# Delta rule's recurrence: four ticks a chunk instead of three, with half ticks between its products

## The chip, the cores and the metric

One Trainium2 chip, one core. The metric is the device time of one execution, in microseconds, over several runs. In the rows of the profile PE is TensorE (PEld its weight loads), DVE VectorE, ACT ScalarE, POOL GpSimd, SP SyncE, whose queue issues the DMAs (SPq).

## The reference, cut to what matters

One decoder layer over 2048 tokens: a projection, two token mixers with four heads each, an output projection, an MLP, a gated embedding. The change concerns one mixer, the gated delta rule. Its state S (128 x 128 for each head) goes from chunk to chunk:

```python
def step(s, inp):
    u_n, w_n, qk_n, qg_n, kt_n, cd_n = inp
    v_new = u_n - w_n @ s                       # u, w: solves of a triangular system of the chunk
    o = qg_n @ s + qk_n @ v_new
    s = s * cd_n + kt_n.T @ v_new
    return s, o
```

The second mixer (HGRN2) has a recurrence of the same kind without the solve.

## The kernel before, in words

All is computed transposed, features by tokens, with tokens in four quarters q of 512. In the mixers' stage (the loop from line 1008 on) the outer work is the input projection: for each quarter one piece "ab" and then, for each of four heads h, eight pieces (`works`). A piece is one bank of 128 x 512 summed over 24 products (line 1020, rows `mm`). It is cut into three *ticks* (`SPT = 3`) of eight products each. After each eight products `tick()` is called: it looks up in `agenda` the generators that are due at this count of the clock, and lets each issue its next step. So the mixers' small products are strewn among the projection's large ones. A head of both mixers starts every 24 ticks (27 where a new quarter starts), and its steps take some 60, so two to three heads are under way at any time.

The gated delta rule's head (`gdn_mixer`, from line 562 on) is such a generator, and the list `A_STEPS` says at which ticks after the head's start its steps are due. In order, with the tick in brackets: load of the decays, keys turned and normed (7 to 9), `kk` products giving u, qk, and the scaled y_kg and y_qg (10), values turned and the store `ud` of the triangular blocks (12), their load `sys` (14), solve of the 32 x 32 blocks on VectorE (16 to 23, tiles pr and xs, lines 653 to 663), store `xd` and loads `xt` (24, 26), transpose to `xn` (28), the merging products psp, psx, psd (30 to 36), then the recurrence, three ticks a chunk, four chunks (38 to 49):

- first product `psa` (line 724): needs the state S; VectorE makes `r` of it (line 726);
- second product `psb` (line 729): needs r; ScalarE makes `w` of it (line 731);
- third product `psc` (line 734): needs w; VectorE makes the next S (line 736); right behind it two products into the output bank `pso` (lines 737, 738).

Each step is one tick from the one before, also psc to the next chunk's psa. After that `finish` (from line 540) takes eight steps (50, 52, 54, 56, 57, 58, 60, 61): og and its squares; the norm's sum `nrm` on TensorE and the DMA `sd`; the load of `m` (line 267); a power of m, on VectorE and GpSimd; the store `rd` (line 273); the broadcast load `rsb` (line 234); the gated og; its store `mixd` (line 555).

Steps of several heads share a tick: at a head's ticks 40 to 47 the next head's solve (its 16 to 23) is due, at 38 the next head's sys load, at 60 and 62 the ud store and the sys load of the head after next. The second mixer's head (`hgrn_mixer`) runs its levels at 24 to 38, a turn at 40, its own recurrence at 42 to 45 and its finish from 46 (`B_STEPS`). The very last head, (3,3), has lists of its own (`A_LAST`, `B_LAST`). After the last piece the clock goes on with tiles of an embedding, six products each, a tick behind each.

TensorE's order is the program's, written by hand as above, and in this stage so is SP's. The order of VectorE, ScalarE and GpSimd is made by a planner that runs through the program with its own costs and issues what is ready; it may bring work forward. SP issues its DMAs strictly in order and waits at each for its data or buffer; the weights of each piece are reloaded (`w`, line 180) at the piece's start, once the piece three before has freed the buffer.

## Time and profile before

| | |
|---|---|
| median of 3 runs | 2773.16 us (2772.43 to 2774.76) |
| the profiled execution's own time | 2769.21 us |
| its span, first to last instruction | 2767.3 us |
| mean granted TensorE clock | 0.993 |
| TensorE busy, share of the span | 2680.7 us, 97% |
| VectorE busy | 2044.9 us, 74% |
| ScalarE busy | 1469.9 us, 53% |
| DMA, mean | 213 GB/s |

A row of a timeline gives the start, the duration, engine, line, operation and what is written from what; in brackets the idle time of the engine just before and what ended it. Successive matmuls overlap in the pipeline, so their distance is read from start to start. A row of the waits gives who waited for whom: total in us, times, longest.

### The profile page before, as it was taken

Reading aid. Unit: us, or ns where it says so; the run is one execution under the profiler, and the core shown is the slowest. Engines: PE = TensorE matmul, PEld = TensorE weight load, DVE = VectorE, ACT = ScalarE, POOL = GpSimd, SP = SyncE. Lnnn points to the kernel's source line nnn. Section 1 sums busy time; section 2 is a strip of 40 time slices with the busy share of each in tenths; the row PEclk is TensorE's granted clock in tenths of the full one; section 3 lists DMA queues with packets and bytes.
Section 4 is the critical chain, followed back from the end, with each engine's and each line's share of the span. In section 5 each row is a group of like instructions: output and inputs, shape, how many; then the busy total and the mean of one; then the engine's idle time right before and its main releaser. Section 6 shows DMA issues by size and latency. Waiting matters only on the chain.

```text
span 2767.3 us, 38374 instructions
## 1 busy us (share of the span) xinstructions
PE 2680.7 (97%) x12721; PEld 2215.3 (80%) x12721; DVE 2044.9 (74%) x4242; ACT 1469.9 (53%) x2943; POOL 104.2 (4%) x104
## 2 busy tenths in 40 slices
PE   6999999999999999999999999999999999999999
PEld 4788788788888887777788888887888888887887
DVE  6788877787787677578889867857787765567775
ACT  6665555455546445575555646545454445465431
POOL 0000000000000000000000000001000000001000
PEclk9999999999999999999999999999999999999999
DMA  7776777667666665887466447667454356577663
GB/s 261 255 250 217 235 247 247 219 209 250 220 213 202 214 227 170 278 276 258 140 214 224 172 175 237 225 193 239 157 191 162 135 175 203 194 254 240 214 206 121
DMA packets 268598, 589.24 MB, mean 213 GB/s; under 512 B 55642, under 2 KB 59960, under 8 KB 249200
## 3 DMA queue, kind: packets, MB, share of 16 engines
q1 hardware_dynamic: 268400, 586.79, 63.6%
q8 instruction: 101, 1.65, 0.3%
q14 instruction: 97, 0.79, 0.1%
HBM read 419.75 MB, written 166.92 MB: 212 GB/s over the span
## 4 chain that ended last, share of the span: by engine, by line
PE 61%; DVE 15%; DMA 10%; issue 7%; ACT 4%; SPq 1%; POOL 1%; DVEq 0%; POOLq 0%; ACTq 0%
PE u L1090 22%; PE d L1090 20%; PE mm L1020 9%; PE mmg L1090 6%; DVE pr_g L658 2%; DMA ud_g<-u_g 2%; DMA sys_g<-ud_g 2%; DVE xs_g L661 1%; DVE xs_g L663 1%; PE mmo L1090 1%; DMA raw_out<-in_w_out_dram 1%; DVE xt L160 1%; DMA rd_g<-m_g 1%; DMA cache_in<-w 1%; DMA rsb_g<-rd_g 1%
## 5 line engine op out<-in xcount | busy, mean ns | idle before, releaser
L1020 PE MATMUL mm<-xt,w 128*128 128x512 f32 x3072 | 770.0, 399 | 3.3 <-ACT qk_h L758 1.6
L1020 PEld LDWEIGHTS mm<-xt,w 128*128 128x128 f32 x3072 | 559.5, 189 | 109.8 <-ACT qk_h L758 2.0
L1090 PE MATMUL d<-db,da 128*128 128x512 f32 x2688 | 615.3, 391 | 5.6 <-ACT db L212 3.7
L1090 PE MATMUL u<-t,wu 128*128 128x512 f32 x2604 | 603.7, 393 | 3.3 <-ACT wu L159 3.3
L1090 PEld LDWEIGHTS d<-db,da 128*128 128x128 f32 x2688 | 506.3, 189 | 113.9 <-ACT db L212 5.0
L1090 PEld LDWEIGHTS u<-t,wu 128*128 128x128 f32 x2604 | 488.7, 188 | 117.6 <-ACT wu L159 4.1
L213 DVE TENSOR_TENSOR db<-db 128x512 fp32r<-128x512 f32 x224 | 161.4, 720 | 75.2 <-ACT db L212 74.3
L1419 DVE TENSOR_TENSOR u<-u,u 128x512 f32<-128x512 f32 x224 | 150.3, 682 | 71.8 <-PE u L1090 70.6
L212 ACT ACTIVATE db<-db 128x512 fp32r<-128x512 f32 x224 | 140.8, 629 | 83.2 <-DMA db<-hid 77.8
L1090 PE MATMUL mmo<-mixT,w_out 128*128 128x512 f32 x720 | 171.7, 399 | 8.9 <-DVE w_out L160 6.4
L1090 PE MATMUL mmg<-h2T,wg 128*128 128x512 f32 x768 | 177.4, 393 | 0.0
L1460 ACT ACTIVATE u<-u 128x512 f32<-128x512 f32 x128 | 80.8, 632 | 176.4 <-DVE u L1419 176.1
L1090 PEld LDWEIGHTS mmo<-mixT,w_out 128*128 128x128 f32 x720 | 137.1, 191 | 42.5 <-DVE w_out L160 8.2
L1090 PEld LDWEIGHTS mmg<-h2T,wg 128*128 128x128 f32 x768 | 144.2, 188 | 32.9
L160 DVE TENSOR_TENSOR da<-da 128x512 fp32r<-128x512 f32 x128 | 93.0, 727 | 87.1 <-ACT da L159 86.9
L159 ACT ACTIVATE da<-da 128x512 fp32r<-128x512 f32 x128 | 80.4, 628 | 134.9 <-DMA da<-sumd 111.3
L159 ACT ACTIVATE wu<-a 128x512 fp32r<-128x512 f32 x124 | 73.9, 622 | 50.6 <-DMA a<-in_w_up_dram 49.2
L658 DVE TENSOR_TENSOR pr_g<-xs_g,sys_g 128x16 f32<-128x16 f32 (+14 forms) x240 | 93.8, 391 | 5.3
L223 POOL TENSOR_TENSOR acc_y<-acc_y,sq_y 128x512 f32<-128x512 f32 x28 | 38.5, 1374 | 1392.8 <-ACT sq_y L222 1392.0
L160 DVE TENSOR_TENSOR wu<-a,wu 128x512 fp32r<-128x512 f32 x124 | 84.7, 686 | 3.6 <-ACT wu L159 3.5
L1461 ACT ACTIVATE u<-u 128x512 f32<-128x512 f32 x128 | 80.8, 631 | 3.7
L160 DVE TENSOR_TENSOR da<-dr,da 128x512 fp32r<-128x512 f32 x96 | 66.2, 690 | 18.5 <-ACT da L159 16.8
(374 smaller groups left out, 3800.9 us busy)
## 6 DMA issues: line engine op xcount, KB each, us to landing
w<-cache_in SPq DMA_DIRECT2D x96, 1024.0 KB
db<-hid SPq DMA_DIRECT2D x224, 256.0 KB
cache_in<-w SPq DMA_DIRECT2D x32, 1024.0 KB
hid<-u SPq DMA_DIRECT2D x128, 256.0 KB
da<-sumd SPq DMA_DIRECT2D x128, 256.0 KB
a<-in_w_up_dram SPq DMA_DIRECT2D x124, 256.0 KB
hid<-ht SPq DMA_DIRECT2D x96, 256.0 KB
dr<-in_w_down_dram SPq DMA_DIRECT2D x96, 256.0 KB
```

What stands on the lines that cost most here:

```text
L159: S.activation(t[:, 0], raw, AF.Copy)
L160: eng.tensor_tensor(t[:, 1], raw, t[:, 0], ALU.subtract)
L212: S.activation(t[:, 0], plain(t), AF.Copy)
L213: V.tensor_tensor(t[:, 1], plain(t), t[:, 0], ALU.subtract)
L223: eng.tensor_tensor(acc, acc, sq, ALU.add)
L658: V.tensor_tensor(pr[:, :, :, 0:i], xs[:, None, :, 0:i].broadcast_to([P, 2, GC, i]), sys[:, 0:i, i : i + 2].rearrange("p j two -> p two j" ...
L661: V.tensor_reduce(xs[:, :, i : i + 2].rearrange("p g two -> p two g"), pr[:, :, :, 0 : i + 1], AX.X, ALU.add)
L1020: PE.matmul(ps, *terms[i], start=i == 0, stop=i == nt - 1)
L1090: PE.matmul(ps, a, b, start=start, stop=stop)
L1419: V.tensor_tensor(c[new], c[old], ps, ALU.add)
L1460: S.activation(c[k], c[k], AF.Relu)
L1461: S.activation(c[k], c[k], AF.Square)
```

## The change

A chunk takes four ticks. psa stands at a whole tick, psb one and a half ticks later, psc one tick after psb, and the next psa one and a half ticks after psc; the four chunks stand at 38, 42, 46 and 50. The finish follows from 53 to 64 with the distances it had. So that a step can be due at a half, `half()` lets the steps of the clock less a half go; it is called in the middle of each eight products, and in the tail, where embedding tiles take the place of the pieces, right before each tick. The lists of the last head are as they were.

```diff
 A_STEPS = ((3, 6, 7, 8, 9, 10, 12, 14) + tuple(range(16, 24)) + (24, 26, 28, 30, 32, 34, 36)
-           + tuple(range(38, 50)) + (50, 52, 54, 56, 57, 58, 60, 61))
+           + tuple(o for c in range(38, 54, 4) for o in (c, c + 1.5, c + 2.5))
+           + (53, 55, 57, 59, 60, 61, 63, 64))
...
         clock[0] += 1
+
+    def half():
+
+        for gen in agenda.pop(clock[0] - 0.5, ()):
+            next(gen, None)
...
                 for s in range(SPT):
                     for i in range(s * nt // SPT, (s + 1) * nt // SPT):
+                        if i == (2 * s + 1) * nt // (2 * SPT):
+                            half()
                         PE.matmul(ps, *terms[i], start=i == 0, stop=i == nt - 1)
...
                     next(outs, None)
+                half()
                 tick()
```

## The prediction

> **What bounds the kernel now.** I read the page first, then the busy time of the stage that the change touches (145 to 1145 us: the recurrences of all sixteen heads, of which the change touches fifteen), then who waits for whom there, and last the timelines of single heads. A head is called by (q, h), times are us from the span's start.

> ```profile
> PE 2680.7 (97%) x12721; PEld 2215.3 (80%) x12721; DVE 2044.9 (74%) x4242; ACT 1469.9 (53%) x2943; POOL 104.2 (4%) x104
> ```
> ```profile
> 145.00:1145.00 1000.00, 966.84 (x5302) 823.16 (x5301) 769.33 (x2193) 541.93 (x1375) 56.25 (x63) 1.00 0.68 224
> ```
> TensorE sets the time: busy for 97% of the span, at the full granted clock in this stage (the 1.00). The change moves products of TensorE but adds and removes none, so all it can win or lose is TensorE's idle time. In the stage that is 1000 less 966.84, 33 us (second row; columns after the window: its length, then busy time of PE, PEld, DVE, ACT, POOL). VectorE is busy for 77% there.

> ```profile
> PE psb_g L729 <- DVE r_g L726: 17.3, 18, 2.6
> ...
> PE psa_g L724 <- DVE S_g L736: 4.5, 4, 1.5
> PE psp_g L682 <- DVE xn_g L677: 2.4, 3, 0.8
> ```
> These rows give the total wait, its count and the longest. Two thirds of the 33 us are the recurrence's own: psb waits for r (17.3) and psa for the state (4.5), both made by VectorE. TensorE takes its products in order, so behind a waiting psb stand all the projection's products. psc, which waits for ScalarE's w, is not in the list at all.

> **What a wait costs, and the distances.** Head (2,1) runs almost without waits:

> ```profile
> 743.37 0.39 PE L734 MATMUL psc_g<-w_g,kt_g 128*128 128x128 f32 x2
> 743.60 0.39 PE L737 MATMUL pso_g<-y_qg,S_g 128*128 128x128 f32 x2
> ...
> 746.34 0.38 PE L724 MATMUL psa_g<-S_g,y_kg 128*128 128x128 f32 x2
> 746.48 2.07 PE L1020 MATMUL mm<-xt,w 128*128 128x512 f32 x8
> 748.39 0.39 PE L729 MATMUL psb_g<-r_g,xt_full 128*128 128x128 f32 x2
> ...
> 762.73 0.39 PE L724 MATMUL psa_g<-S_g,y_kg 128*128 128x128 f32 x2
> ```
> Two small products take 0.22 to 0.23 from start to start, and psa to psb, with a tick's eight large products between, 2.05; so a half tick (four) is 0.92. Breaking the stream once more costs nothing that these rows show: 2.05 is 0.22 and eight products of 0.229. For the 120 places in fifteen heads that move to a half tick I take zero (bounds: 0.02 us either way at each, 2.4 us in all). The eight large products (start 746.48, 2.07) overlap the next start by 0.16, so a wait loses 0.16 more than its idle time, and 0.10 more in the restart (0.49 against 0.39 in the waits below): 22 waits, 21.8 + 22 x 0.26 = 27.5 us. That is the most that can be won.

> **What goes.** Some waits are a distance a little too short. One of chunk 0, in (0,3), TensorE and VectorE:

> ```profile
> 342.74 0.39 PE L724 MATMUL psa_g<-S,y_kg 128*128 128x128 f32 x2
> ...
> 347.65 0.49 PE L729 MATMUL psb_g<-r_g,xt_full 128*128 128x128 f32 x2 [0.94 <-DVE r_g L726]
> ```
> ```profile
> 347.26 0.34 DVE L726 SCALAR_TENSOR_TENSOR r_g<-vt_g,inv_g,psa_g 128x128 f32<-128x128 f32 x1
> ```
> psb can start 0.39 after r starts, here 4.91 after psa. Undisturbed the distance is 2.5 (psa's pair 0.22, four small products of a level 0.44, eight large ones 1.83), with the half tick 3.4: 1.5 stays. Others are of another kind. (3,0), again TensorE and VectorE, and VectorE's total wait of this sort in the stage:

> ```profile
> 938.22 0.39 PE L734 MATMUL psc_g<-w_g,kt_g 128*128 128x128 f32 x2
> ...
> 945.66 0.49 PE L729 MATMUL psb_g<-r_g,xt_full 128*128 128x128 f32 x2 [1.34 <-DVE r_g L726]
> ...
> 960.35 0.39 PE L724 MATMUL psa_g<-S_g,y_kg 128*128 128x128 f32 x2
> ```
> ```profile
> 940.01 0.23 DVE L663 SCALAR_TENSOR_TENSOR xs_g<-xs_g,sys_g 128x4 f32<-128x4 f32 x1 [2.96 <-DMA sys_g<-ud_g]
> ...
> 959.77 0.34 DVE L736 SCALAR_TENSOR_TENSOR S_g<-S_g,cd_g,psc_g 128x128 f32<-128x128 f32 x1
> ```
> ```profile
> DVE xs_g L663 <- DMA sys_g<-ud_g: 21.6, 11, 3.5
> ```
> VectorE stood still for 2.96 us because sys_g, the next head's triangular blocks, had not landed; then it works through the next head's solve without a pause, and r and S lie in that row of work. Five heads, (0,1), (0,2), (1,1), (1,2) and (3,0), are late in this way. To them belong the four waits of psa (4.5) and five of psb, the last of them the 1.34 above, together by my reading about 7.4: with 0.26 for each of the nine, 14.2 of the 27.5.

> In these five the half tick helps little, because VectorE, not the distance, sets the pace up to about tick 47. Old: chunk 0's psc to chunk 3's psa (ticks 40 to 47) takes 19.36 in (2,1) and 22.13 in (3,0); 2.77 are lost. New: chunk 2's psa stands at tick 46, its psb at 47.5. Up to that psb TensorE has the same work as up to old chunk 3's psa, less a psb (0.22) and a psc with its two outputs (0.67, three pairs), plus a half tick (0.92): 19.4. Its r takes the place that the state update of tick 46 has in VectorE's row today, 959.77. So psb can't start before 960.16, and its turn is at 938.22 + 19.4 = 957.62: 2.54 is still lost, 0.2 won. The same rows of the other four give 0.2 to 1.1; I take 0.6 for each of the five, 3 in all.

> The waits of the first kind are the remaining 13.3. In the four heads that wait at chunk 0 (the first shown, the last (2,3)) about 2.5 stay; chunk 3's go, since its psb moves from tick 48 to 51.5, when the solve is through; for chunk 2, whose psb now bears the end of the solve, I leave 2.3. Won: 8.5.

> **What is added.** The finish (norm, gate, store) comes three ticks later, with all it issues: the sd store at tick 55, the m load at 57, the rd store at 60, the rsb load at 61, mixd at 64. VectorE's share of it, with chunk 3's r and S, moves into ticks 50 to 53, ahead of the transpose for psp (tick 54). psp's wait of 2.4 could grow; 48 to 62 is where VectorE is least pressed, so I take 1 (bounds 0 and 8, half a microsecond a head). Operands that are needed longer (y_kg to tick 50, rewritten at 52; y_qg to 52.5, rewritten at 55) keep two ticks, 4 us; were that used up, ScalarE's write would wait, not TensorE. In (3,2) the last two chunks fall among the embedding's tiles of six products (1.4 by the 0.229 above), where a half tick stands right before the next tick: 0, at most 1.

> The SP queue is the delicate part. At tick 60 it issues the ud store of the head after next, and at 62 the sys load that was late above. (3,0) today:

> ```profile
> 981.81 0.32 SPq L180 DMA_DIRECT2D w<-cache_in  x1
> 984.55 0.32 SPq L273 DMA_DIRECT2D rd_g<-m_g  x1
> ...
> 987.04 0.32 SPq L234 DMA_DIRECT2D rsb_g<-rd_g  x1
> 991.33 0.32 SPq L180 DMA_DIRECT2D w<-cache_in  x1
> 991.75 1.80 SPq L638 DMA_DIRECT2D ud_g<-u_g  x4
> ...
> 997.21 0.54 SPq L647 DMA_DIRECT2D sys_g<-ud_g  x1
> ```
> ```profile
> 522.62 0.32 SPq L180 DMA_DIRECT2D w<-cache_in  x1
> 523.03 0.38 SPq L273 DMA_DIRECT2D rd_g<-m_g  x1
> ```
> rd (tick 57 today) will stand ahead of ud, behind the weights' reload of tick 60. If m is done by then, as in (1,1) (last two rows), ud is later by one issue, 0.42 (991.33 to 991.75). That is the low end; the high end, 2.7, is a rival. I take 0.42, since m's data are loaded three ticks ahead. The five late heads pay it whole, 2.1; of the other ten half, 2. The rsb load then waits for rd's landing ahead of sys: 987.04 less 984.55 is 2.5, and sys waits 5.5 from ud's issue anyway (991.75 to 997.21), so that is covered.

> Those 5.5 us decide whether sys is late at all. [...] The measured 5.5 decides.

> **Sum.** 3 + 8.5 won, 1 + 2.1 + 2 lost: 6.4 us. The profiled execution took 2769.21; it would take 2763. The median of the runs shown, 2773.16, is 4 us above it, so 2767.

> **Rivals.** *Full relief*: the planner, which orders VectorE's work anew, puts r and S ahead of the solve's steps, and nearly all of the 27.5 goes; less the 5 lost, 2751. For it: a distance of 1.5 ticks exceeds most of the delays. Against it: the solve itself is late. *The wait only moves*: the solve's end decides everywhere, and psb of chunk 2 loses what psb of chunks 1 and 3 lost; 2773, no change. *The SP queue turns it round, slower*: in (3,0) rd is issued 2.74 after the reload of its work (981.81 to 984.55), because m was not done. Moved rigidly by three ticks it keeps ud back by 2.7. sys lands later by as much, and VectorE starts the solve later. The five late heads lose 2.7 each, 13.5. The others have a reserve, in (2,1):

> ```profile
> 761.49 0.34 DVE L736 SCALAR_TENSOR_TENSOR S_g<-S_g,cd_g,psc_g 128x128 f32<-128x128 f32 x1
> ```
> 761.49 + 0.40 against 743.37 + 19.4 leaves 0.9, so ten heads lose 1.8 each, 18. Less the 11.5 won, with the 1 for psp: 21 slower, 2794, if every head meets it; if half do (and half pay the low end), about 7, 2780. I take the middle, 2787. It decides from a delay of about 1.3 us on (5 x 1.3 and 10 x 0.4, and the 1, are the 11.5 won). For it: the rigid shift. Against it: (1,1), where rd follows its reload at once. A change that does nothing is excluded: fifteen heads use these steps; the last has its own.

> **Chances.** Forecast 0.42 (2767, own range 2761 to 2772, 0.25 of it below 2767.6), full relief 0.12, only moved 0.13, SP queue 0.28, another order of VectorE that costs time 0.05. The range 2752 to 2788 leaves out the ends of full relief and of the queue. What a measurement can tell from no change is 0.2%, 5.5 us. Faster by more: 0.25 and full relief, 0.37; within it: the rest of the forecast and the moved waits, 0.30; slower by more: 0.33.

> **What would show it.** Right: psb's wait for r falls from 17.3 to about 9, psa's from 4.5 to under 2, what is left of psb's lies in chunk 2 of the five late heads; the rd store stands less than 1 us behind its reload; VectorE's wait for sys_g stays under 30. Wrong, to the fast side: psb's wait under 4. Wrong, to the slow side: sys_g above 40, ud more than 1.3 us behind the reload, and the waits of psb, psa and psp together above 28.

## The result, and the profile after

The changed kernel takes 2782.38 us (median of six runs, 2779.64 to 2787.36) against 2772.80 for the kernel before (six runs): ratio 1.0029, 95% interval 1.0018 to 1.0039. It is slower by 0.3%, where the prediction said 0.2% faster. The profiled execution took 2780.50 us, span 2778.7 (before 2767.3), mean granted clock 0.990 (before 0.993). It is not one execution alone: the six runs of the changed kernel have a granted clock of 0.988 to 0.991, those of the kernel before in the experiments below, on three chips, 0.991 to 0.996.

Changed lines have moved: psa is L730, r L732, psb L735, w L737, psc L740, S L742; the projection's products are L1028. The page's busy times and the stage from 145 to 1145 us, after:

```profile
PE 2688.3 (97%) x12721; PEld 2223.5 (80%) x12721; DVE 2045.3 (74%) x4242; ACT 1469.2 (53%) x2943; POOL 105.5 (4%) x104
```
```profile
145.00:1145.00 1000.00, 965.13 (x5258) 825.65 (x5257) 765.24 (x2184) 536.07 (x1369) 55.39 (x62) 0.99 0.67 221
```

TensorE runs the same 12721 products but is busy 7.6 us longer, and the stage's granted clock is 0.99 where it was 1.00. TensorE's waits from 145 to 1165 us (total, times, longest; the rows of before that the prediction shows are the same up to 1165):

```profile
PE ps_gb L485 <- DVE gbb L482: 13.0, 3, 4.4
PE pso_h L847 <- DVE S_h L846: 10.8, 9, 2.6
PE at_h L819 <- DVE qk_h L825: 3.1, 1, 3.1
PE psc_g L740 <- ACT w_g L737: 2.8, 5, 0.8
...
PE psa_g L730 <- DVE S_g L742: 1.1, 2, 0.6
...
PE psb_g L735 <- DVE r_g L732: 0.5, 2, 0.3
```

The waits that the change was to shorten are gone: psb's fell from 17.3 to 0.5 us, psa's from 4.5 to 1.1. Two others have come, neither of which stands in the list of before: the second mixer's pso_h waits 10.8 us for its state S_h (more on it below), and ps_gb 13.0 in only three waits. ps_gb belongs to a step not told of so far. `decays` computes a quarter's decays: its first step makes gb with a scan on VectorE, its third copies half of gb into gbb on VectorE (L482) and transposes gb and gbb on TensorE into ps_gb (L485). It is put on the clock from the piece "ab" with the offsets (0, 2, 4, 5), so the third step of quarter q falls on tick 99q + 6. That is tick 54 of head (q-1, 2), whose finish stood at 50 and 52 and now begins at 53 and 55. VectorE, then TensorE, at the first border, after:

```profile
315.73 1.35 DVE L475 TENSOR_TENSOR_SCAN gb<-one,sp 4x128 f32<-4x128 f32 x4
...
318.42 0.66 DVE L551 TENSOR_TENSOR og_g<-pso_g,zt_zg 128x512 f32<-128x512 f32 x1
...
320.60 0.67 DVE L161 TENSOR_TENSOR hl_g<-osq_g,hl_g 128x512 fp32r<-128x512 f32 x1
...
323.25 0.27 DVE L482 COPY gbb<-gb 36x256 f32<-36x256 f32 x1
```
```profile
323.58 0.32 PE L485 MATMUL ps_gb<-cst,gbb 36*128 36x36 f32 x1 [4.32 <-DVE gbb L482]
...
324.04 3.78 PE L1028 MATMUL mm<-xt,w 128*128 128x512 f32 x8
```

The same place before:

```profile
310.59 0.69 DVE L545 TENSOR_TENSOR og_g<-pso_g,zt_zg 128x512 f32<-128x512 f32 x1
...
319.13 1.35 DVE L469 TENSOR_TENSOR_SCAN gb<-one,sp 4x128 f32<-4x128 f32 x4
...
321.58 0.30 DVE L476 COPY gbb<-gb 36x256 f32<-36x256 f32 x1
```
```profile
322.36 0.23 PE L479 MATMUL ps_gb<-cst,gbb 36*128 36x36 f32 x1
```

Before, the finish's og started 8.5 us ahead of the scan, and the transposes ran without a wait. After, gb is ready at 317.1 (315.73 + 1.35), but the planner puts the finish's og, its squares and their split, and with them steps of a convolution and of the second mixer, ahead of the small copy gbb, which starts only at 323.25. Of these 6.2 us the finish's three steps take 1.8; why the planner puts the convolution's, which stood behind the copy before, ahead of it as well, no run shows. TensorE, which takes its products in order, stands for 4.32 us. It waits in the same way at 587.24 (4.35) and 852.94 (4.38).

Then comes what the trace of before does not show in this stage at all. The same border in windows of 3.41 us (start and end, length, busy time of PE, PEld, DVE, ACT, POOL, granted clock, DMA):

```profile
318.09:321.50 3.41, 1.17 (x10) 0.93 (x8) 3.41 (x8) 2.13 (x8) 0.00 (x0) 0.99 1.14 341
321.50:324.91 3.41, 1.33 (x5) 1.17 (x6) 3.07 (x9) 1.97 (x4) 0.00 (x0) 0.50 0.85 294
324.91:328.33 3.42, 3.42 (x9) 2.65 (x9) 3.01 (x7) 0.41 (x2) 0.00 (x0) 0.51 0.84 278
328.33:331.74 3.41, 3.41 (x22) 3.03 (x22) 0.81 (x3) 1.68 (x5) 0.00 (x0) 1.00 0.18 25
```

The clock is halved from 321.50 to 328.33, 6.8 us: the eight large products at 324.04 take 3.78 us, those of the prediction's rows 2.07. Between 70 and 1165 us the kernel before has no such stretch, the changed one has 30.7 us of them: 6.8 at the first and the third border, 3.4 at the second, 3.4 behind pso_h's longest wait at 818.33, and three of 3.4 at 126.9, 1109.9 and 1120.2.

The sum, from the two traces: TensorE's idle time from 70 to 1165 us (stretches over 0.05 us) goes from 36.8 (42 waits) to 39.6 us (31 waits), +2.8. For the halved clock I take, as an estimate, half of the time within the 30.7 us in which TensorE works, +13.1. Outside this stage the same two terms give -3.9 (clock) and +1.1 (idle). The four add up to 13.1, where the spans differ by 11.4; the remaining 1.7 I can't place. So the total wait hardly changed. It was concentrated in fewer and longer waits, and those cost the clock as well.

### The profile page after: what moved, and what is told of

It is laid out like the page before. It is cut to its first block, busy times and chain, and to the rows that moved or that the text cites. A ratio compares the mean times of both kernels' runs of the same rounds, so it can differ in the third digit from the quotient of the medians.

```text
span 2778.7 us, 38391 instructions
## 1 busy us (share of the span) xinstructions
PE 2688.3 (97%) x12721; PEld 2223.5 (80%) x12721; DVE 2045.3 (74%) x4242; ACT 1469.2 (53%) x2943; POOL 105.5 (4%) x104
## 4 chain that ended last, share of the span: by engine, by line
PE 48%; DVE 5%; DMA 3%; ACT 2%; issue 2%; SPq 0%; POOL 0%; DVEq 0%; ACTq 0%; POOLq 0%
PE u L1099 22%; PE d L1099 19%; PE mmg L1099 6%; PE mmo L1099 1%; DMA da<-sumd 1%; DMA xo<-in_xT_dram 0%; DVE w_out L161 0%; DVE t L161 0%; DMA db<-hid 0%; DMA raw_out<-in_w_out_dram 0%; PE mme L187 0%; DMA b<-h1d 0%; ACT da L160 0%; DVE acc_o L224 0%; ACT L1136 0%
## 5 line engine op out<-in xcount | busy, mean ns | idle before, releaser
L1028 PE MATMUL mm<-xt,w 128*128 128x512 f32 x3072 | 796.0, 404 | 2.3 <-ACT qk_h L764 1.6
L1028 PEld LDWEIGHTS mm<-xt,w 128*128 128x128 f32 x3072 | 558.8, 191 | 103.9 <-ACT qk_h L764 2.0
```

The costliest lines, as they stand in the source:

```text
L1028: PE.matmul(ps, *terms[i], start=i == 0, stop=i == nt - 1)
```

## The experiments

Each time is given as a ratio to the kernel before on the same chip, since chips differ (medians of before: 2767.59 for the first four runs, 2772.59 for the next three, 2768.59 for the last two).

**The border's copy alone: two ticks later.** The third and fourth step of `decays` are moved out of the finish's way, from the second quarter on.

```diff
-                        at(clock[0], decays(ps, q), (0, 2, 4, 5))
+                        at(clock[0], decays(ps, q), (0, 2, 6, 7) if q else (0, 2, 4, 5))
```

> The changed kernel with one shift: the step of the quarter's decays that copies gbb and turns ps_gb comes two ticks later (from the second quarter on), away from the tick at which the moved finish puts its norm on VectorE. Theory A (the recurrence's waits are gone, but VectorE's row at the quarter's border is fuller, TensorE waits 4.3 us for gbb three times, and its clock is halved behind these waits): the three ps_gb waits (13.0 us) fall under 3, the half-clock stretches at 321, 588 and 850 go, the time falls by 15 to 20 us, to 2762 to 2768, below the kernel before. Theory B (breaking the large products' stream at half ticks costs about 0.1 us at each of 120 places, 10 us in all): only the 13 us of wait go, less what moves on, 2770 to 2773. Theory C (SP's queue, rd ahead of ud): nothing at the border matters, 2778 to 2783.

Measured: 2759.13 us, ratio 0.9968 (0.9956 to 0.9981). The waits from 145 to 1165 us, and the place at the first border:

```profile
PE pso_h L847 <- DVE S_h L846: 7.3, 7, 1.9
```
```profile
321.00 0.28 DVE L482 COPY gbb<-gb 36x256 f32<-36x256 f32 x1
```
```profile
322.45 0.23 PE L485 MATMUL ps_gb<-cst,gbb 36*128 36x36 f32 x1
```

ps_gb's waits are gone, idle time is 22.9 us, the halved clock 10.2. The copy comes no sooner: it starts 7.9 us behind the scan (313.13 to 321.00), in the changed kernel 7.5; it is TensorE that comes to it later. One pair of offsets in another function turns the change from 0.3% slower to 0.3% faster than the kernel before. psb's and psa's waits stay as small as in the changed kernel (0.5 and 0.9), so the recurrence keeps its gain, and it was the border that took it back.

**The late finish alone.** The kernel before, with its old recurrence, but the finish three ticks later:

```diff
-           + tuple(range(38, 50)) + (50, 52, 54, 56, 57, 58, 60, 61))
+           + tuple(range(38, 50)) + (53, 55, 57, 59, 60, 61, 63, 64))
```

> The kernel before with its recurrence at ticks 38 to 49, and only the finish moved to 53 to 64. Theory A: the recurrence's waits for r and S stay (about 22 us), the wait for gbb at the three borders comes (8 to 13 us) and the clock falls behind it: 10 to 20 us slower than before, 2783 to 2793. Theory B: no half ticks, so no slower, 2771 to 2775. Theory C: the queue order is that of the changed kernel, so 8 to 12 us slower, but with sys_g later and no wait for gbb.

Measured: 2778.1 us, ratio 1.0034 (1.0021 to 1.0046), as slow as the whole change, with no half tick in it.

```profile
PE psb_g L729 <- DVE r_g L726: 18.7, 25, 1.6
PE psp_g L682 <- DVE xn_g L677: 5.6, 4, 2.3
...
PE ps_gb L479 <- DVE gbb L476: 2.4, 1, 2.4
```

The collision takes different forms at the three borders: ps_gb waits 2.38 at 320.30, psp 2.28 at 582.92 and 2.29 at 844.72. Idle time is 38.6 us, only 1.8 more than before, and the clock is halved for 13.7 us (318.9 to 325.8 and 844.6 to 851.4). So psp's wait, which the prediction had named, does grow, but at the borders, not in every head. With psp's 0.8 at the first border the waits at the borders are 7.8 us, against 2.4 before (psp alone) and 13.0 in the changed kernel: the late finish makes a collision by itself, but not the whole of it. Nor is the equal time made up in the same way: here psb's waits have stayed.

**Control: the same shift in the kernel before.**

> Control for the first run: the kernel before with the decays' step two ticks later. All theories: its ps_gb waits are 4.6 us in two cases, so 0 to 5 us faster, 2768 to 2773. If it gains as much as the first run, that run says nothing of the finish.

Measured: 2766.56 us, ratio 0.9994 (0.9985 to 1.0002). The shift gains nothing that can be told where the finish does not stand in its way. (The 4.6 us that the expectation counts are two waits of quarter 0, at 61.6 and 64.7 us, which the shift leaves as they are; at the borders ps_gb did not wait before.) So the 0.3% of the first experiment are the change's own, not the shift's.

**Work in place of the wait.** The changed kernel, with 24 products of a size that fills the wait, whose result nothing reads, ahead of the border's transposes:

```diff
             ps = bank(f"ps_gb_{q}", ph)
+            for i in range(24 if q else 0):
+                PE.matmul(ps[:, NC * 36 :], xts[q][i % KD][:, 0, :P], xts[q][i % KD][:, 1, NC * 36 :],
+                          start=True, stop=True)
```

> The changed kernel with 24 products of 368 columns (about 4 us of TensorE's time, results read by nobody) ahead of ps_gb at the three borders, so that TensorE is busy where it waited for gbb. Theory A: the wait is as long but is no idling, the half-clock stretches at 321, 588 and 850 (17 us, 8.5 us of loss less what the wait covers) go, so 3 to 8 us faster than the changed kernel, 2774 to 2779, although work was added. If the clock had no part: the same as the changed kernel or slower, 2780 to 2786.

Measured: 2771.42 us, ratio 1.0014 (1.0002 to 1.0026).

```profile
317.65 4.25 PE L485 MATMUL ps_gb<-xt 128*128 128x368 f32 x24
...
322.50 0.25 PE L488 MATMUL ps_gb<-cst,gbb 36*128 36x36 f32 x1 [0.42 <-DVE gbb L482]
```

The border takes as long as with the wait (4.25 of work and 0.42 against 4.32), and the halved clock goes from 30.7 to 3.4 us. So it is TensorE's idling that is followed by the halved clock, not the border's length. The time is 1.0014 against 1.0029, some 4 us less, with intervals that overlap; by the sum above it should be 11, and the last projection product starts 5.8 earlier (1089.4 against 1095.2). That the clock stays up is shown; that this saves time is likely, and its size stays open.

**Half the shift.** One tick instead of two:

```diff
-                        at(clock[0], decays(ps, q), (0, 2, 4, 5))
+                        at(clock[0], decays(ps, q), (0, 2, 5, 6) if q else (0, 2, 4, 5))
```

> The changed kernel with the decays' last two steps one tick later (offsets 0, 2, 5, 6) instead of two. If the border's wait is a distance: a tick with its products (2 us) comes off each of the three waits of 4.3 to 4.4, leaving 2 to 2.5 each, and the clock is halved behind those of the three whose idle time falls by more than 1.7 us into one of the gate's windows of 3.4 us (none of the nine traces so far has a halved stretch begin behind less than 1.72, or a full one go on behind more than 1.69): ratio 0.998 to 1.001, between 1.0029 and 0.9968. If the gain of the two ticks comes from another order on VectorE and not from the distance: the waits stay at 4 and the ratio at 1.003, or they vanish at once and the ratio is 0.997.

Measured: 2762.73 us, ratio 0.9980 (0.9971 to 0.9989).

```profile
PE ps_gb L485 <- DVE gbb L482: 4.7, 3, 1.6
```
```profile
319.41:322.82 3.41, 1.84 (x11) 1.47 (x11) 3.03 (x11) 2.90 (x5) 0.00 (x0) 1.00 1.04 316
322.82:326.24 3.42, 3.42 (x15) 3.13 (x14) 2.71 (x6) 1.03 (x4) 0.00 (x0) 0.50 1.05 292
```

It lies between, as a distance would: each of the three waits is 1.57 us, 2.8 less for one tick. Behind two of the three the clock was halved (322.8 and 582.2), behind the third (842.26) not. Ahead of the first of them stood 1.57 us of idle time in one window (3.41 less 1.84), less than the 1.7 that the expectation gives. No run shows the gate that it speaks of; what the traces show of its windows stands in the last section.

**Do the halves matter?** With the shift, the recurrence on whole ticks:

```diff
-           + tuple(o for c in range(38, 54, 4) for o in (c, c + 1.5, c + 2.5))
+           + tuple(o for c in range(38, 54, 4) for o in (c, c + 2, c + 3))
```

> The changed kernel with the decays' shift (offsets 0, 2, 6, 7 from the second quarter on), and in it the recurrence on whole ticks: psa at c, psb at c + 2, psc at c + 3, the next psa at c + 4. Tells whether the halves matter or only that a chunk has four ticks. If the distance of each pair of products decides: psb's wait for r stays under 1 us, but psc to the next psa is one tick again, as in the kernel before, where psa lost 4.5 us, so psa loses 3 to 5 and the ratio to the kernel before is about 0.998. If only the four ticks count (the solve ends by then, whichever product waits): psa under 1.5 us and the ratio 0.9968 as with the halves. If breaking the eight products in the middle costs 0.1 us each, which the late finish alone spoke against: 0.993.

Measured: 2758.05 us, ratio 0.9949 (0.9930 to 0.9967).

```profile
PE psa_g L730 <- DVE S_g L742: 8.9, 12, 2.2
...
PE pso_h L847 <- DVE S_h L846: 2.9, 2, 1.5
```

psa's wait comes back, more than expected (8.9 us), and pso_h's goes down by 4.4; idle time is 23.7 us against 22.9 with halves. The two can't be told apart in time. A chunk's fourth tick counts, and where in it the products stand does not show.

**The second recurrence spread.** With the shift and the halves:

```diff
-B_STEPS = (..., 38, 40, 42, 43, 44, 45, 46, ...)
+B_STEPS = (..., 38, 40, 41, 42.5, 44, 45.5, 46, ...)
```

> The changed kernel with the decays' shift, and the second mixer's recurrence spread from ticks 42, 43, 44, 45 to 41, 42.5, 44, 45.5. If pso_h's wait for S_h (7.3 us with the shift alone) is a distance too short by about a half tick: it falls under 3, the halved clock behind it at 803 us goes, and the ratio is 0.995. If S_h is late because VectorE is behind with its whole row: the wait stays at 5 to 8 and the ratio at 0.9968.

Measured: 2761.07 us, ratio 0.9963 (0.9951 to 0.9975).

```profile
PE psc_g L740 <- ACT w_g L737: 5.3, 5, 2.3
PE psa_g L730 <- DVE S_g L742: 3.6, 6, 1.2
...
PE psb_g L735 <- DVE r_g L732: 2.9, 6, 0.9
...
PE pso_h L847 <- DVE S_h L846: 0.9, 2, 0.5
```

pso_h's wait goes as expected (7.3 to 0.9), the time does not: psc, psa and psb lose 11.8 us where they lost 4.0. So pso_h's wait was a distance too short, and the waits change places; halved stretches in the stage, 3.4 us where there were 10.2, and idle time, 26.8 where it was 22.9, about cancel.

**The old steps in head (3,2), whose end lies in the tail**, added to this:

```diff
                 a_steps, b_steps = (A_LAST, B_LAST) if (q, h) == (NQ - 1, 3) else (A_STEPS, B_STEPS)
+                if (q, h) == (NQ - 1, 2):
+                    a_steps = A_OLD
```

> As the one with the spread second recurrence, and head (3,2), whose last two chunks fall among the embedding's tiles, takes the steps of the kernel before. If the two stretches of halved clock in the tail (3.4 us each near 1086 and 1096 us) come of the three ticks that its finish is later there: they go, and the ratio is lower by 0.001 (some 3 us) than without. If they come of the last head alone: no difference.

Measured: 2760.04 us, ratio 0.9959 (0.9943 to 0.9974). The last halved stretch of the stage, behind at_h's wait of 3.1 us, goes. The gain of 0.001 that was expected can't be told at these intervals.

**All together, on whole ticks.**

> Everything found so far together: four ticks a chunk on whole ticks (psa c, psb c + 2, psc c + 3), the decays' shift (0, 2, 6, 7), the second recurrence at 41, 42.5, 44, 45.5, and the steps of the kernel before in head (3,2). If what each took away stays away: no halved clock between 70 and 1165 us, TensorE idle under 22 us there, ratio 0.9945. If the waits only change places, as they did with the spread second recurrence alone: idle 23 to 27 and ratio 0.996, no better than the shift alone.

Measured: 2754.48 us, ratio 0.9948 (0.9936 to 0.9961), the lowest found beside the whole ticks' 0.9949, 0.5% below the kernel before and 0.8% below the change as it was made (0.9948 / 1.0029).

```profile
145.00:1145.00 1000.00, 976.54 (x5353) 832.68 (x5352) 779.23 (x2200) 544.64 (x1386) 55.63 (x64) 1.00 0.68 227
```

Idle time from 70 to 1165 us is 27.8, in 39 waits of which none is over 1.9, and no stretch of halved clock lies between 71 and 1165 us: more wait than with the shift alone, and no more time. The idle time that I expected (under 22) did not come; the ratio did. That it beats the shift alone (0.9968) is not shown, since the intervals overlap.

## Why the prediction was wrong, step by step

- **What can be won.** Nearly all of psb's and psa's 21.8 us of waiting went, but not all of that was won. psc and pso_h, which did not wait before, wait 13.6 together, and 9.9 with the border freed (the first experiment). So the 21.8 became 15.2, and 11.3 there. In the late heads VectorE does set the pace, as forecast, but what is left of the wait does not stand in front of psb. In (3,0), from the start of tick 40 (938.22 in the prediction's rows; now the second mixer's turn t_hkh, since psc stands half a tick later):

```profile
947.67 0.60 PE L538 MATMUL t_hkh<-cst,qk_h 128*128 128x128 f32 x4
...
956.44 0.49 PE L847 MATMUL pso_h<-qk_h,S_h 128*128 128x128 f32 x2 [0.85 <-DVE S_h L846]
...
969.00 0.49 PE L735 MATMUL psb_g<-r_g,xt_full 128*128 128x128 f32 x2 [0.20 <-DVE r_g L732]
```
```profile
948.69 0.23 DVE L669 SCALAR_TENSOR_TENSOR xs_g<-xs_g,sys_g 128x4 f32<-128x4 f32 x1 [2.19 <-DMA sys_g<-ud_g]
...
956.04 0.34 DVE L846 SCALAR_TENSOR_TENSOR S_h<-S_h,gg_h,pss_h 128x128 f32<-128x128 f32 x1
...
968.60 0.34 DVE L732 SCALAR_TENSOR_TENSOR r_g<-vt_g,inv_g,psa_g 128x128 f32<-128x128 f32 x1
```

  VectorE's row from the solve's start to r takes 19.91 us, where the row to the state update took 19.76 (940.01 to 959.77): it stayed, as assumed, and r comes 0.6 earlier, since the solve starts 0.77 earlier against tick 40 (1.02 behind it, before 1.79). psb starts 21.33 behind tick 40, so 1.9 are lost against the undisturbed 19.4, where the forecast had 2.54. But only 0.20 of them are psb's own wait.

  TensorE had been held up before, mainly at pso_h, which needs S_h, and S_h is made in the same row of VectorE. Before, psc and its outputs stood between two steps of the second mixer, 3.19 us from one to the next (945.99 to 949.18); moved away, they leave 2.53 (952.67 to 955.20), and S_h comes too late. The spread second recurrence, which lengthens this distance, bears it out (7.3 to 0.9).

  Over all fifteen heads TensorE takes 309.4 us from tick 40 to psb of chunk 2, where it took 304.8 before to the product in that place (psa of chunk 3), and 305.8 with the border freed. So in these ticks nothing was won, and the rival *the wait only moves* was right there, with another product than it named; what was won lies at chunks 0 and 3, the waits of the first kind. The 3 us for the five late heads were too many by the traces of before as well: worked like (3,0), the other four give 0.0 to 0.5 each, not 0.2 to 1.1.
- **The finish's move, 1 us (bounds 0 and 8).** This is the step that failed and, with the clock, turned the sign. The prediction looked at who waits for VectorE in ticks 50 to 53 of the same heads (psp, which it put at 1 and whose wait went from 2.4 to 0.5) and called those ticks the least pressed. It did not list the steps of other generators at 53 to 57: the gbb copy of `decays`, once a quarter, with TensorE behind it. That is 13.0 us of waiting in three places, outside the bounds. With the copy's step out of the way the changed kernel is 8.5 us faster than the kernel before (7.4 faster than the kernel before with the same shift), where 6.4 were forecast; that it comes so near is in part luck, since the terms of that sum did not come out one by one.
- **The clock.** The 1.00 of the stage was quoted and then taken as given. The waits were priced at their idle time and 0.26 each, read from waits of which none had halved the clock. The term that was missing comes to 13.1 us, by the estimate above.
- **The SP queue.** The rival that ended on the slow side was not the mechanism. In (3,0) rd stands right behind its reload, and ud behind rd, at the low end of the bounds; of the other heads from 345 us on, three have ud 1.6 to 2.2 behind the reload, the rest under 1:

```profile
1000.00 0.32 SPq L181 DMA_DIRECT2D w<-cache_in  x1
1000.37 0.42 SPq L274 DMA_DIRECT2D rd_g<-m_g  x1
1000.88 1.94 SPq L644 DMA_DIRECT2D ud_g<-u_g  x4
```
```profile
DVE xs_g L669 <- DMA sys_g<-ud_g: 16.1, 12, 3.6
```

  VectorE's wait for sys_g fell from 21.6 to 16.1; the prediction's bound of 30 held. The 5.5 us that it reads from ud's issue to sys are not all ud's landing: the four issues of ud take 1.8 of them, and two other stores hold the queue up to 995.87, so that sys could have gone 1.3 earlier at most.
- **The half ticks at nothing.** Nothing speaks against it: with the border freed the kernel with half ticks is 8.5 us faster than the kernel before, and the whole ticks are not measurably better.
- **Head (3,2) in the tail, 0, at most 1.** at_h waits 3.1 us there, with a halved stretch behind it. With the old steps in this head that wait goes, but another of the tail's comes back (mme for ScalarE's sq_e, 1.5 to 5.0), and the time can't be told apart.
- **The signs named beforehand.** Psb under 4 was to be the sign of the fast side. It came true, and the kernel was slower: the signs watched the waits that the change touches, and the time went to waits of other heads' steps and to the clock. A rival "the wait moves to another generator's step" was missing; the *wait only moves* of the prediction had it at the solve's end.

## What to carry over

A step that is moved takes all its work on every engine past the steps of whatever else is due at those ticks: list these, the rare ones too (here a copy once a quarter), and ask of each what TensorE has queued behind it. Waits on a busy TensorE need not be worth their sum: from 70 to 1165 us the kernel before has 42 of them, 36.8 us, the longest 2.60, and no halved clock; the changed one has 31, 39.6 us, three of them of 4.3 to 4.4, and 30.7 us of halved clock. So a change that leaves the total as it is and concentrates it can be slower. A product taken out of a tick shortens that tick for the others in it, whose own waits may then appear (here 3.19 us became 2.53, and pso_h's waits came). And where a wait vanishes, count the waits behind the same engine's work before calling it won: here about half of it stood in front of another product.

## What the runs showed of the hardware

The length of a wait does not tell in these traces whether a halved stretch follows; what goes with it is how much of one window is idle. The traces of before and after, from 70 to 1165 us, have 631 windows at full clock. In seven of them, all in the changed kernel, TensorE is idle for 1.9 to 3.1 us, and a halved window follows each; in the others it is idle for 1.7 at most, and none follows. Less was followed by one in the late finish alone, 1.78 (3.41 less 1.63, from 315.50 to 318.91), and in half the shift, the 1.57 above. So these runs give no one limit. The two longest waits of pso_h in the changed kernel show how a wait falls into windows:

```profile
550.08:553.49 3.41, 1.79 (x9) 1.32 (x7) 3.34 (x9) 1.26 (x2) 0.00 (x0) 1.00 0.66 246
553.49:556.90 3.41, 2.65 (x15) 2.30 (x16) 3.41 (x8) 0.37 (x1) 0.00 (x0) 1.00 0.73 216
```
```profile
816.41:819.82 3.41, 1.49 (x9) 1.33 (x10) 3.41 (x9) 0.63 (x1) 0.00 (x0) 1.00 0.33 110
819.82:823.24 3.42, 3.42 (x14) 3.03 (x13) 2.16 (x7) 1.03 (x3) 0.00 (x0) 0.50 1.02 329
```

A wait of 2.38 us, ending at 554.25, fell across a border of windows, and TensorE was still busy for 1.79 and 2.65 of them: the clock stayed at 1.00. One of 2.62, ending at 818.33, left 1.49 busy in one window: the next was halved. In the kernel before, psb's longest wait, 2.60 us, ending at 288.53, lay across a border at 287.18, and the clock stayed at 1.00 in both windows, 2.15 and 2.07 of them busy; with the decays' shift in that kernel the same wait, 2.27 long, lay within one window, and the clock was halved from 288.9 to 292.3. So waits of 2.38 and 2.60 us had no halved clock behind them, and waits of 2.27 and 2.62 had: what differs between the two pairs is where they lay on the grid. Whether this makes part of the scatter between runs was not shown. No experiment of its own varied how much of a window is idle.
